# Two hybrid decoder layers on one core: the decay rate's group ahead of the receptance, a denser inverse, and a recurrence issued without gates

## The chip, the cores and the metric

The kernel runs on 1 core of one Trainium2 chip. The metric is the device time of one execution in microseconds (us). The engines are named as in the profile: PE is TensorE, DVE is VectorE, ACT is ScalarE, POOL is GpSimd, and SP issues most of the DMAs. PEld is TensorE's weight load.

## The reference

Two layers act on x of 256 tokens by 2048 features. Each layer makes one projection of x and splits its columns among three token mixers and their gates; the outputs go through one output projection, a residual and a layer norm.

```python
for l in range(DEPTH):
    u = x @ w_in[l]
    (cb, cc, ch, cg, cq, ckv, kpe, mg, rcols, rg) = _split(u, IN_SIZES)
    y_conv = _short_conv_branch(cb, cc, ch, cg, conv_w[l])
    y_mla = _mla_branch(cq, ckv, kpe, mg, ...)
    y_rwkv = _rwkv7_branch(rcols, rg, ...)
    mix = jnp.concatenate([y_conv, y_mla, y_rwkv], axis=-1)
    x = _layer_norm(DEEPNORM_ALPHA * x + mix @ w_out[l], ln_g[l], ln_b[l])
```

The third mixer, RWKV-7, is the one that the change is about. From rcols come the receptance r, the key k, the value v, a decay w and a removal rate a; 8 heads of 64 keep a 64x64 state each:

```python
def step(state, inp):
    r_t, w_t, k_t, v_t, a_t, b_t = inp
    sa = jnp.einsum('bhvk,bhk->bhv', state, a_t)
    state = (state * w_t[:, :, None, :] + sa[..., None] * b_t[:, :, None, :]
             + v_t[..., None] * k_t[:, :, None, :])
    return state, jnp.einsum('bhvk,bhk->bhv', state, r_t)
```

## The kernel before

**Projections.** The input projection is computed in groups of 512 columns, in the order of the tuple MAIN (k, r, a, v, cq, cc, ch, cb, cg, rg), later the two groups of LATE (mg). The group called a holds the inputs of decay and removal rate (64 columns each) with the latent key and value inputs. Apart from k, a group is two half-groups of 256 columns, and a half-group is four quarters of 16 matmuls (L437 and L439). Every weight is split into a high part (`hi_...`, a cast on ScalarE) and a low part (`lo_...`, a subtraction on VectorE); both are held in rings of four buffers, and the raw weights, which SP loads, in a ring of five. The accumulators of the groups (`u_...`, `pkv`, `pq`, `po`) share a ring of two.

**Ticks.** Other work is written as generators (rwkv, latent, conv). After each quarter, `tick` resumes every generator up to its next `yield`. While it does so, VectorE's instructions that are issued through the wrapper `V` are gated: `gates` makes each stand behind the low split of the weights two quarters ahead. `tc.high_priority(AHEAD)` and `tc.high_priority(EVICT)` rank instructions ahead of others. From these ranks and a timeline of its own, the scheduler sets the order on each engine.

**RWKV.** rwkv_k normalises the key (`kx`, `kkn`); rwkv_r makes the shifted receptance `rx`; rwkv_decay computes decay and rate with two small products (`pw`, `pa`, L569 and L570), a tanh each (`sig`, `tha`) and a scan (`cum`), from which `pe` and `pinv` come; rwkv_scale makes the scaled operands `kp`, `bk` and `ar`. The 256 tokens are four chunks of 64. rwkv_products multiplies within chunks (`pg`) and masks into `gs`. rwkv_inverse inverts 64 triangular blocks of 32x32: `gs` goes through DRAM into `bt`, then 31 steps of two VectorE instructions run (`tm`, then an addition into `xi`), and `xi` goes through DRAM into `xq`, is transposed (`xt1`) and merged into 64x64 inverses (`pz`, `zs`, `px`). rwkv_pairs (`pk`, `pv`, `pq` with `qs`) runs beside it.

rwkv_chain is the recurrence over chunks. For each chunk after the first it multiplies the state (`prh`), adds `qs` (`rhs`), multiplies by the inverse (`pu`) and copies the result into `uvt`, then makes the next state (`pst`, `st`); `out` makes the outputs of two chunks (`py`), which ScalarE copies to `y`. rwkv_norm begins with a sum over `y` (`gm`).

**Behind rg.** After rg the keys and values of the latent attention are expanded (mla_kv: `pkv`, evicted to `kn`, `vs`, `vt`), then the queries (mla_q: `pq`, `qn`, and `qp` by rope with the temporary `rt_q`), then mg is projected while mla_attend works head by head (`sc`, `ptr`, `po`).

Of the kernel before, what the change touches and what calls it, by code (L numbers as in the profile page):

```python
# [10 lines left out]
F32 = mybir.dt.float32  # L11
# [3 lines left out]
ALU = mybir.AluOpType  # L15
AX = mybir.AxisListType

P = 128
D = 2048
S = 256  # L20
# [4 lines left out]
AHEAD = 1500  # L25
EVICT = 4000
# [85 lines left out]
def hybrid_layers(ctx: ExitStack, tc: tile.TileContext, x, positions, xT, w_in, w_out, w_uq, w_ukv, par, wa_in, gb_in,  # L112
                  gbp, cst, eye32, sums, out):
    nc = tc.nc
# [8 lines left out]
    sm = ctx.enter_context(tc.tile_pool(name="sm", bufs=2))  # L123
    dr = ctx.enter_context(tc.tile_pool(name="dr", bufs=1, space=bass.MemoryType.DRAM))

    gates, splits = {}, []
# [18 lines left out]
    V, A, G, T = Gated(nc.vector, "V"), Gated(nc.scalar, "A"), nc.gpsimd, nc.tensor  # L145
# [151 lines left out]
    def until(name):  # L297
        while name not in done:
            yield
# [44 lines left out]
        for i, src in enumerate((hi, lo)):  # L344
            T.matmul(o, ones[:, which * P:which * P + P], src, start=i == 0, stop=i == 1)

    MAIN, LATE, ORDER = ("k", "r", "a", "v", "cq", "cc", "ch", "cb", "cg", "rg"), ("mg0", "mg1"), (0, 12, 4, 8)

    def acc(name):

# [126 lines left out]
    def rwkv(l, pq, u, t):  # L477
        yield from until(f"k{l}")
        yield from rwkv_k(l, pq, t, u["k"][0])
        yield from until(f"r{l}")  # L480
        yield from rwkv_r(l, pq, t, u["r"][0])
        yield from until(f"a{l}")
        yield from rwkv_decay(l, pq, t, u["a"][0][0])
        yield from rwkv_scale(l, pq, t)
        yield from rwkv_products(l, t)
        inv = rwkv_inverse(l, t)
        while f"v{l}" not in done:
            next(inv)
            yield
        yield from rwkv_v(l, pq, t, u["v"][0])  # L490
        fill = rwkv_pairs(l, t)
        while True:
            a, b = next(inv, "end"), next(fill, "end")
            if a == b == "end":
                break
            yield
        yield from rwkv_chain(l, t)
        done.add(f"chain{l}")
        yield from rwkv_norm(l, pq, t)
        yield from until(f"heads{l}")  # L500
        yield from rwkv_gate(l, t)
# [166 lines left out]
    def rwkv_inverse(l, st):  # L668
        gs = st["gs"]
        bd = dr.tile([64, 32, 32], F32, tag=f"bd{l}", name=f"bd{l}")  # L670
        for par in range(2):
            for k in range(2):
                r = slice(par * 64 + k * 32, par * 64 + k * 32 + 32)
                u0 = (par * 2 + k) * 16
                for i in range(2):
                    src = gs[i].rearrange("p c (b q) t -> p c b q t", q=2)[r, :, :, par, k * 32:k * 32 + 32]
                    nc.sync.dma_start(bd[u0 + 8 * i:u0 + 8 * i + 8].rearrange("(c b) i j -> i c b j", b=4), src)
        bt = s4(f"bt{l}", (64, 32, 32))
        nc.sync.dma_start(bt, bd)
        xi = s4(f"xi{l}", (64, 32, 32))  # L680
        after(nc.sync.dma_start(xi, eye32.rearrange("p (i j) -> p i j", j=32)), st["mark"])
        yield
        yield
        yield
        n = 0
        for j in range(31, 0, -1):
            w = 32 - j
            tm = sm.tile([64, j, w], F32, tag="rt", name=f"tm{l}_{j}")
            V.tensor_tensor(tm, bt[:, 0:j, j:j + 1].to_broadcast([64, j, w]),
                            xi[:, j:j + 1, j:32].to_broadcast([64, j, w]), ALU.mult)  # L690
            V.tensor_tensor(xi[:, 0:j, j:32], xi[:, 0:j, j:32], tm, ALU.add)
            n += 1
            if n == 3:
                yield
                n = 0
        xd = dr.tile([64, 32, 32], F32, tag=f"xd{l}", name=f"xd{l}")
        nc.sync.dma_start(xd, xi)
        xq = s4(f"xq{l}", (P, 4, 4, 64))
        xt1 = sm.tile([P, 4, 4, 32], F32, tag="s", name=f"xt1{l}")
        V.memset(xq, 0.0)  # L700
        yield
        for par in range(2):
            for k in range(2):
                r = slice(par * 64 + k * 32, par * 64 + k * 32 + 32)
                u0 = (par * 2 + k) * 16
                nc.sync.dma_start(xq[r, :, :, k * 32:k * 32 + 32],
                                    xd[u0:u0 + 16].rearrange("(c b) i j -> i c b j", b=4))
        yield
        yield
        for par in range(2):  # L710
            r = slice(par * 64, par * 64 + 32)
            t1 = V.transpose(xt1[r].rearrange("p c b t -> p (c b) t"), xq[r, :, :, 0:32].rearrange("p c b t -> p (c b) t"))
        yield
        zs = sm.tile([P, 16, 32], F32, tag="s", name=f"zs{l}")
        quarters = [(slice(par * 64, par * 64 + 32), slice(par * 64 + 32, par * 64 + 64)) for par in range(2)]
        pz = [pm.tile([P, 16, 32], F32, tag="m", name=f"pz{l}_{par}") for par in range(2)]
        for c in range(4):
            for b in range(4):
                for par, (ra, rb) in enumerate(quarters):
                    m = T.matmul(pz[par][rb, c * 4 + b, :], gs[c // 2][ra, c % 2, 2 * b + par, 32:64],  # L720
                                 xt1[ra, c, b, :], start=True, stop=True)
                    if c == b == par == 0:
                        gather(m, [t1])
        for par, (ra, rb) in enumerate(quarters):
            z1 = V.tensor_copy(zs[rb], pz[par][rb])
        yield
        px = [pm.tile([P, 16, 32], F32, tag="m", name=f"px{l}_{par}") for par in range(2)]
        for c in range(4):
            for b in range(4):
                for par, (ra, rb) in enumerate(quarters):  # L730
                    m = T.matmul(px[par][ra, c * 4 + b, :], zs[rb, c * 4 + b, :], xq[rb, c, b, 32:64],
                                 start=True, stop=True)
                    if c == b == par == 0:
                        gather(m, [z1])
        for par, (ra, rb) in enumerate(quarters):
            st["xq1"] = V.tensor_copy(xq[ra, :, :, 32:64].rearrange("p c b t -> p (c b) t"), px[par][ra])
        yield
        st["xq"] = xq
# [47 lines left out]
    def rwkv_chain(l, st):  # L786
# [28 lines left out]
        for c in range(4):  # L815
            cc = slice(c * 64, (c + 1) * 64)
            if state is None:
                rhs = qs[:, 0]
            else:
                pr_ = pm.tile([P, 4, 64], F32, tag="m", name=f"prh{l}_{c}")  # L820
                for b in range(4):
                    for par in range(2):
                        T.matmul(pr_[rs[par], b, :], ar[rs[par], b, 0, cc], state[rs[par], b, :], start=True, stop=True)
                rhs = slot("rhs", f"rhs{l}_{c}", (P, 4, 64), 2)
                V.tensor_tensor(rhs, pr_, qs[:, c], ALU.add)
                yield
            pu = pm.tile([P, 4, 64], F32, tag="m", name=f"pu{l}_{c}")
            for b in range(4):
                for par in (1, 0):
# [3 lines left out]
            moved = []  # L833
            for par in range(2):
                dst = uvt[:, c].rearrange("p (b q) t -> p b q t", q=2)[rs[par], :, par, :]
                if par == 0:
                    moved.append(V.tensor_copy(dst, pu[rs[par]]))
                else:
                    moved.append(A.copy(dst, pu[rs[par]]))
            yield  # L840
            if c < 3:
                pst = pm.tile([P, 4, 64], F32, tag="m", name=f"pst{l}_{c}")
                for b in range(4):
                    for par in (1, 0):
                        h = 2 * b + par
                        m = T.matmul(pst[rs[par], b, :], bkt[:, c, h, :], uvt[:, c, h, :], start=True, stop=True)
                        if b == 0 and par:
                            gather(m, moved)
                new = slot("st", f"st{l}_{c}", (P, 4, 64), 2)
                pc_ = pe[:, c::4, 64:65].to_broadcast([P, 4, 64])  # L850
                if state is None:
                    V.tensor_tensor(new, pst, pc_, ALU.mult)
                else:
                    V.tensor_tensor(new, pst, state, ALU.add)
                    V.tensor_tensor(new, new, pc_, ALU.mult)
            before.append(state)
            if c % 2:
                out(c // 2, before[-2:], moved)
# [196 lines left out]
    def mla_attend(l, st):  # L1055
# [4 lines left out]
        def split_queries(h):  # L1060
            t = qk[h % 2]
            split_in(t[:, 0, 0:P], t[:, 1, 0:P], qn[:, h, P:S])
# [3 lines left out]
            split_queries(h)  # L1066
            split_keys(st, h)

        split_queries(0)
        for par in range(2):  # L1070
            r, o = halves[par], halves[1 - par]
            of = lambda rr: q1.rearrange("p (g q) t -> p q g t", q=2)[rr, par]
            A.copy(of(r), qp[r, :, P:S])
            V.tensor_tensor(of(o), qp[r, :, P:S], of(r).bitcast(F32), ALU.subtract)
        split_queries(1)
        yield
        live = {}
        both = ((0, slice(0, 128)), (1, slice(128, 384)))

# [361 lines left out]
```

## Time and profile before

| | |
|---|---|
| median of 3 runs | 926.83 us (926.5 to 927.11) |
| profiled execution | 927.77 us |
| its span, first to last instruction | 926.0 us |
| mean granted clock of TensorE in it | 0.986 |
| busy: PE, DVE, ACT, POOL | 902.3, 690.7, 483.7, 22.7 us |
| HBM read, written | 158.61, 5.32 MB |

A busy time is a sum over the span, and an engine can be busy at a lower clock: the row PEclk of the profile gives the granted clock of TensorE in tenths, in 40 slices of the span, 9 standing for 90% or more. In a row of waits, the figures behind the colon are the sum in us over the execution, the number of times and the longest. In a row of a timeline, the first two figures are start and duration in us, the shapes are output and inputs, and the bracket gives the idle time of that engine just before and what ended it. In a row of windows, each engine has its busy time and its instructions, then come PEclk, the DMA engines' share and GB/s.

### The profile page before, as it was taken

To read this page: it belongs to the slowest core of one execution; us is meant where nothing else is said; L and a number is where in the kernel's file an instruction comes from. 1 tells how busy PE (TensorE), PEld (TensorE's weight loads), DVE (VectorE), ACT (ScalarE), POOL (GpSimd) and SP (SyncE) were. 2 spreads that over 40 slices of the span, in tenths; PEclk is the share of its full clock that TensorE was granted. 3 is DMA by queue.
4 is the path that set the end of the run, shared out by engine and by line. 5 is a ranking of instruction groups with operands and counts; after the bars stand their busy time and mean duration, and the time that the engine had idled before them with its cause. 6 is when DMAs were issued, how large, how long until landed. Compare 5 with 4: busy or idle time off the path is not lost.

```text
span 926.0 us, 15967 instructions
## 1 busy us (share of the span) xinstructions
PE 902.3 (97%) x6311; PEld 792.7 (86%) x6311; DVE 690.7 (75%) x1166; ACT 483.7 (52%) x750; POOL 22.7 (2%) x47
## 2 busy tenths in 40 slices
PE   8999999999989999999999999999999899999996
PEld 7888888888879888788898888888888898987896
DVE  6786898886548977566765778999865499763865
ACT  5756636444446566444246576464444366754430
POOL 1210000000000000000020000000000000000000
PEclk9999999999989999999999999999999799999998
DMA  9866465667434654596486664656664256546942
GB/s 319 257 177 213 122 188 163 178 185 202 149 86 122 192 160 137 158 343 206 159 227 185 185 181 147 185 142 190 191 178 142 70 160 189 151 136 191 338 131 91
DMA packets 67547, 164.97 MB, mean 178 GB/s; under 512 B 15430, under 2 KB 24694, under 8 KB 67462
## 3 DMA queue, kind: packets, MB, share of 16 engines
q1 hardware_dynamic: 59712, 150.36, 54.0%
q10 hardware_dynamic: 5072, 9.57, 3.1%
q0 software_dynamic: 2688, 4.03, 1.6%
q8 instruction: 49, 0.80, 0.4%
q14 instruction: 26, 0.21, 0.1%
HBM read 158.61 MB, written 5.32 MB: 177 GB/s over the span
## 4 chain that ended last, share of the span: by engine, by line
PE 90%; DVE 5%; ACT 1%; issue 1%; DMA 1%; SPq 0%; ACTq 0%; DVEq 0%
PE u_mg L437 6%; PE po L337 6%; PE po L338 6%; PE po L339 6%; PE u_rg L437 3%; PE u_cc L437 3%; PE u_cg L437 3%; PE u_cb L437 3%; PE u_mg L439 3%; PE u_ch L437 3%; PE u_v L437 3%; PE u_a L437 3%; PE u_cq L437 3%; PE u_r L437 3%; PE u_cc L439 2%; PE u_cg L439 2%
## 5 line engine op out<-in xcount | busy, mean ns | idle before, releaser
L138 DVE TENSOR_TENSOR lo_wo<-w_wo,hi_wo 128x1024 fp32r<-128x1024 f32 x57 | 69.2, 1222 | 52.0 <-ACT hi_wo L138 51.1
L138 ACT CAST hi_wo<-w_wo 128x1024 fp32r<-128x1024 f32 x57 | 59.6, 1053 | 65.4 <-PE po L339 49.2
L437 PE MATMUL u_mg<-x,hi_mg 128*128 128x512 f32 x256 | 90.8, 397 | 0.7 <-DVE rt_q L138 0.7
L439 PE MATMUL u_mg<-x,lo_mg 128*128 128x256 f32 x256 | 71.6, 280 | 0.0
L437 PEld LDWEIGHTS u_mg<-x,hi_mg 128*128 128x128 f32 x256 | 48.1, 188 | 11.7 <-issue 1.1
L337 PE MATMUL po<-hi_wo,ma 128*128 128x512 f32 (+1 forms) x128 | 46.8, 365 | 2.1 <-ACT ma L138 2.1
L439 PEld LDWEIGHTS u_mg<-x,lo_mg 128*128 128x128 f32 x256 | 48.3, 188 | 0.0
L138 ACT CAST hi_mg<-w_mg 128x1024 fp32r<-128x1024 f32 x32 | 33.6, 1050 | 26.5 <-PE pq L338 9.0
L339 PE MATMUL po<-hi_wo,ma 128*128 128x512 f32 (+1 forms) x128 | 46.6, 364 | 0.0
L437 PE MATMUL u_rg<-x,hi_rg 128*128 128x512 f32 x128 | 46.5, 404 | 0.0
L338 PE MATMUL po<-lo_wo,ma 128*128 128x512 f32 (+1 forms) x128 | 46.5, 363 | 0.0
L437 PE MATMUL u_cc<-x,hi_cc 128*128 128x512 f32 x128 | 46.5, 400 | 0.0
L437 PE MATMUL u_r<-x,hi_r 128*128 128x512 f32 x128 | 45.4, 397 | 0.9 <-DVE kx L138 0.9
L437 PE MATMUL u_cg<-x,hi_cg 128*128 128x512 f32 x128 | 45.7, 400 | 0.0
L138 DVE TENSOR_TENSOR lo_mg<-w_mg,hi_mg 128x1024 fp32r<-128x1024 f32 x32 | 39.1, 1221 | 8.8 <-ACT hi_mg L138 8.6
L437 PE MATMUL u_cb<-x,hi_cb 128*128 128x512 f32 x128 | 45.3, 399 | 0.0
L437 PE MATMUL u_ch<-x,hi_ch 128*128 128x512 f32 x128 | 45.3, 399 | 0.0
L437 PE MATMUL u_cq<-x,hi_cq 128*128 128x512 f32 x128 | 45.1, 396 | 0.0
L437 PE MATMUL u_v<-x,hi_v 128*128 128x512 f32 x128 | 44.9, 392 | 0.0
L437 PE MATMUL u_a<-x,hi_a 128*128 128x512 f32 x128 | 44.5, 391 | 0.0
L339 PE MATMUL u_k<-x,lo_k 128*128 128x256 f32 x128 | 36.6, 286 | 1.0 <-DVE lo_k L138 1.0
L337 PE MATMUL u_k<-x,hi_k 128*128 128x256 f32 x128 | 36.9, 288 | 0.6 <-ACT hi_k L138 0.6
(414 smaller groups left out, 2818.5 us busy)
## 6 DMA issues: line engine op xcount, KB each, us to landing
w_wo<-in_w_out_dram SPq DMA_DIRECT2D x64, 512.0 KB, 4.3
w_mg<-in_w_in_dram SPq DMA_DIRECT2D x32, 512.0 KB, 4.2
w_r<-in_w_in_dram SPq DMA_DIRECT2D x16, 512.0 KB, 5.6
w_a<-in_w_in_dram SPq DMA_DIRECT2D x16, 512.0 KB, 3.8
w_v<-in_w_in_dram SPq DMA_DIRECT2D x16, 512.0 KB, 4.0
w_cq<-in_w_in_dram SPq DMA_DIRECT2D x16, 512.0 KB, 3.7
w_cc<-in_w_in_dram SPq DMA_DIRECT2D x16, 512.0 KB, 3.9
w_ch<-in_w_in_dram SPq DMA_DIRECT2D x16, 512.0 KB, 3.8
```

Of the source, the lines that this page charges most:

```text
L138: inst = call(*args, **kwargs)
L337: m = T.matmul(o, lh, rh, start=first, stop=False, skip_group_check=True)
L338: T.matmul(o, lh, rl, start=False, stop=False, skip_group_check=True)
L339: T.matmul(o, ll, rh, start=False, stop=last, skip_group_check=True)
L437: T.matmul(ps[:, b, :].rearrange("p (i t) -> p i t", i=2), hi[:, k, c], x2, start=k0 + k == 0, stop=False, skip_group_check=True)
L439: T.matmul(ps[:, b, 0:S], lo[:, k, c], x2[:, 0, :], start=False, stop=k0 + k == NKC - 1, skip_group_check=True)
```

## The change

MAIN has the group a ahead of r, and rwkv runs rwkv_decay ahead of rwkv_r. The inverse does five steps between two yields, where it did three, and its `tm` is taken from the pool tag "s" (which `xt1` and `zs` use) and no longer from "rt" (which the norms' temporaries use). In the recurrence the yield behind `rhs` is gone, so a chunk takes two ticks where it took three, and its VectorE instructions are issued on the engine itself, without the gate, at priority EVICT. In mla_attend the gates are cleared for the first tick, and the splits of the first queries are ranked AHEAD.

```diff
-    MAIN, LATE, ORDER = ("k", "r", "a", "v", "cq", "cc", "ch", "cb", "cg", "rg"), ("mg0", "mg1"), (0, 12, 4, 8)
+    MAIN, LATE, ORDER = ("k", "a", "r", "v", "cq", "cc", "ch", "cb", "cg", "rg"), ("mg0", "mg1"), (0, 12, 4, 8)
...
         yield from rwkv_k(l, pq, t, u["k"][0])
+        yield from until(f"a{l}")
+        yield from rwkv_decay(l, pq, t, u["a"][0][0])
         yield from until(f"r{l}")
         yield from rwkv_r(l, pq, t, u["r"][0])
-        yield from until(f"a{l}")
-        yield from rwkv_decay(l, pq, t, u["a"][0][0])
...
-            tm = sm.tile([64, j, w], F32, tag="rt", name=f"tm{l}_{j}")
+            tm = sm.tile([64, j, w], F32, tag="s", name=f"tm{l}_{j}")
...
-            if n == 3:
+            if n == 5:
                 yield
...
-                V.tensor_tensor(rhs, pr_, qs[:, c], ALU.add)
-                yield
+                with tc.high_priority(EVICT):
+                    nc.vector.tensor_tensor(rhs, pr_, qs[:, c], ALU.add)
...
-                if par == 0:
-                    moved.append(V.tensor_copy(dst, pu[rs[par]]))
-                else:
-                    moved.append(A.copy(dst, pu[rs[par]]))
+                with tc.high_priority(EVICT):
+                    moved.append((A.copy if par else nc.vector.tensor_copy)(dst, pu[rs[par]]))
...
-                if state is None:
-                    V.tensor_tensor(new, pst, pc_, ALU.mult)
-                else:
-                    V.tensor_tensor(new, pst, state, ALU.add)
-                    V.tensor_tensor(new, new, pc_, ALU.mult)
+                with tc.high_priority(EVICT):
+                    if state is None:
+                        nc.vector.tensor_tensor(new, pst, pc_, ALU.mult)
+                    else:
+                        nc.vector.tensor_tensor(new, pst, state, ALU.add)
+                        nc.vector.tensor_tensor(new, new, pc_, ALU.mult)
...
-        split_queries(0)
-        for par in range(2):
...
-        split_queries(1)
-        yield
+        gates.clear()
+        with tc.high_priority(AHEAD):
+            for par in range(2):
...
+                split_queries(par)
```

The change moves instructions on all engines. At three places the order reads as follows; the number behind a name's first underscore is the layer's or the chunk's, and the last number only tells tiles apart.

TensorE at the end of the recurrence in layer 0. Before, behind the second group of keys and values, the last steps stand one after another:

```order
L338 MATMUL pkv0_1_2968<-lo_ukv0_1_0_2884,hkv0_1481 128x256
L339 MATMUL pkv0_1_2968<-hi_ukv0_1_0_2883,hkv0_1481 128x256
L846 MATMUL pst0_2_2439<-uvt0_1554,bkt0_1458 64x64 x8
L823 MATMUL prh0_3_2473<-st0_2_2448,ar0_1058 64x64 x8
L830 MATMUL pu0_3_2506<-rhs0_3_2482,xq0_1979 64x64 x8
L799 MATMUL py0_1_0_2542<-uvt0_1554,gs0_1_1166 64x64 x8
```

Now `pst` of chunk 2 stands 22 matmuls of rg earlier, and `prh` of chunk 3 comes at the beginning of the first group:

```order
L437 MATMUL u_rg0_1_2814<-x0_3_85,hi_rg0_1_12_2839 128x512
L439 MATMUL u_rg0_1_2814<-x0_3_85,lo_rg0_1_12_2840 128x256
L337 MATMUL pkv0_0_2933<-hkv0_1561,hi_ukv0_0_0_2861 128x256
L338 MATMUL pkv0_0_2933<-hkv0_1561,hi_ukv0_0_0_2861 128x256
L339 MATMUL pkv0_0_2933<-hkv0_1561,lo_ukv0_0_0_2862 128x256
L823 MATMUL prh0_3_2281<-st0_2_2249,ar0_988 64x64 x8
```

`pu` of chunk 3 follows 21 matmuls of that group later, and `py` behind the 24 of the second.

ScalarE behind the recurrence, where it evicts the first two groups of keys and values (`vs`, `vt`) and the last outputs (`y`). Before:

```order
L138 CAST vs0_2926<-pkv0_0_2933 128x256
L138 CAST vs0_2926<-pkv0_1_2968 128x256
L138 COPY vt0_2925<-pkv0_0_2933 128x256
L138 COPY vt0_2925<-pkv0_1_2968 128x256
L138 COPY y0_2190<-py0_1_0_2542 128x4x64
L138 COPY y0_2190<-py0_1_1_2543 128x4x64
L138 ACTIVATE gsq0_2605<-y0_2190 128x1024
```

Now:

```order
L138 CAST vs0_2926<-pkv0_0_2933 128x256
L138 CAST vs0_2926<-pkv0_1_2968 128x256
L138 COPY y0_2039<-py0_1_0_2331 128x4x64
L138 COPY y0_2039<-py0_1_1_2332 128x4x64
L138 COPY vt0_2925<-pkv0_0_2933 128x256
L138 COPY vt0_2925<-pkv0_1_2968 128x256
L138 ACTIVATE gsq0_2396<-y0_2039 128x1024
```

The two copies of `y` have moved ahead of the two of `vt`.

VectorE in the inverse of layer 0, between two low splits of weights. Before, in ch:

```order
L138 TENSOR_TENSOR lo_ch0_1_8_1924<-w_ch0_1_8_1921,hi_ch0_1_8_1923 128x1024
L138 TENSOR_TENSOR tm0_17_1789<-bt0_1454,xi0_1456 64x255
L138 TENSOR_TENSOR xi0_1456<-xi0_1456,tm0_17_1789 64x17x15
L138 TENSOR_TENSOR tm0_16_1815<-bt0_1454,xi0_1456 64x256
L138 TENSOR_TENSOR lo_ch0_1_12_1955<-w_ch0_1_12_1952,hi_ch0_1_12_1954 128x1024
```

Now, in cc:

```order
L138 TENSOR_TENSOR lo_cc0_1_8_1697<-w_cc0_1_8_1694,hi_cc0_1_8_1696 128x1024
L138 TENSOR_TENSOR tm0_22_1598<-bt0_1387,xi0_1389 64x220
L138 TENSOR_TENSOR xi0_1389<-xi0_1389,tm0_22_1598 64x22x10
L138 TENSOR_TENSOR tm0_21_1646<-bt0_1387,xi0_1389 64x231
L138 TENSOR_TENSOR xi0_1389<-xi0_1389,tm0_21_1646 64x21x11
L138 TENSOR_TENSOR tm0_20_1649<-bt0_1387,xi0_1389 64x240
L138 TENSOR_TENSOR xi0_1389<-xi0_1389,tm0_20_1649 64x20x12
L138 TENSOR_TENSOR lo_cc0_1_12_1740<-w_cc0_1_12_1737,hi_cc0_1_12_1739 128x1024
```

Three steps stand between two splits where there was one and a half, and the same steps come in an earlier group.

More of the change, by code (lines that the diff above doesn't have):

```diff
@@ L1067, in split_qk @@
             split_keys(st, h)
-        split_queries(0)
-        for par in range(2):
[L1071 to L1074, printed above, removed]
-        split_queries(1)
-        yield
+        gates.clear()
+        with tc.high_priority(AHEAD):
+            for par in range(2):
+                r, o = halves[par], halves[1 - par]
+                of = lambda rr: q1.rearrange("p (g q) t -> p q g t", q=2)[rr, par]
+                A.copy(of(r), qp[r, :, P:S])
+                V.tensor_tensor(of(o), qp[r, :, P:S], of(r).bitcast(F32), ALU.subtract)
+                split_queries(par)
         live = {}
```

## The prediction

> **What bounds the kernel now.** I read the page first, then who waits on TensorE, then TensorE's timeline where the waits lie, then the granted clock in half-microsecond windows there. The page's head:
>
> ```profile
> span 926.0 us, 15967 instructions
> PE 902.3 (97%) x6311; PEld 792.7 (86%) x6311; DVE 690.7 (75%) x1166; ACT 483.7 (52%) x750; POOL 22.7 (2%) x47
> PEclk9999999999989999999999999999999799999998
> ```
>
> TensorE is busy 97% of the span, so at most 23.7 us of idle time are to be had. But the clock row dips twice inside (0.8 and 0.7 of a slice of 23 us), and there a busy TensorE works at half speed. The waits of TensorE, both layers summed:
>
> ```profile
> PE prh L823 <- DVE st L138: 3.5, 2, 1.7
> PE u_cq L439 <- DVE lo_cq L138: 1.3, 2, 0.7
> PE pu L830 <- DVE rhs L138: 1.1, 2, 0.5
> ```
>
> Two of them belong to the recurrence (prh, pu). They lie where its last chunk comes after the last half-group of the gate, rg, with nothing left to put between the steps. TensorE there, layer 0, columns start, duration, instruction:
>
> ```profile
> 261.70 0.28 PE L337 MATMUL pkv<-hkv,hi_ukv 128*128 128x256 f32 x1
> 261.82 0.28 PE L338 MATMUL pkv<-hkv,hi_ukv 128*128 128x256 f32 x1
> ...
> 268.35 0.69 PE L846 MATMUL pst<-uvt,bkt 128*64 128x64 f32 x16
> 270.76 0.68 PE L823 MATMUL prh<-st,ar 64*64 64x64 f32 x16 [1.73 <-DVE st L138]
> 271.97 1.02 PE L830 MATMUL pu<-rhs,xq 64*64 64x64 f32 x16 [0.53 <-DVE rhs L138]
> 272.92 1.71 PE L799 MATMUL py<-uvt,gs 128*64 128x64 f32 x18
> ...
> 277.83 0.58 PE L337 MATMUL pkv<-hkv,hi_ukv 128*128 128x256 f32 x1 [0.28 <-ACT vt L138]
> ...
> 301.27 0.35 PE L337 MATMUL pq<-hq,hi_uq 128*128 128x256 f32 x1 [0.26 <-DVE rt_q L138]
> ...
> 306.18 0.47 PE L437 MATMUL u_mg<-x,hi_mg 128*128 128x512 f32 x1 [0.37 <-DVE rt_q L138]
> ```
>
> A pkv matmul starts every 0.12 us at 261.7. And the clock (first column the window, the figure behind POOL is PEclk):
>
> ```profile
> 272.00:272.50 0.50, 0.50 (x12) 0.50 (x14) 0.00 (x0) 0.00 (x0) 0.40 (x1) 0.62 0.82 326
> 282.00:282.50 0.50, 0.50 (x5) 0.50 (x4) 0.00 (x0) 0.50 (x1) 0.00 (x0) 0.64 0.00 0
> 729.50:730.00 0.50, 0.11 (x4) 0.00 (x0) 0.34 (x1) 0.00 (x0) 0.00 (x0) 0.51 0.96 197
> 739.50:740.00 0.50, 0.50 (x5) 0.50 (x5) 0.14 (x1) 0.27 (x1) 0.00 (x0) 0.75 0.00 0
> 390.00:392.00 2.00, 0.94 (x5) 0.44 (x4) 1.20 (x2) 1.89 (x3) 0.00 (x0) 1.00 0.73 170
> ```
>
> In each layer the clock falls to 0.50 right after the recurrence's waits. With the share of the edge windows it is low from about 272.2 to 282.4 and from 729.5 to 739.8, 10.2 us each. At 390 to 392, TensorE is idle for half of the window and the clock stays at 1.00.
>
> [...]
>
> **The change, part by part.** The profiled execution took 927.77 us with a span of 926.0; it stands 0.94 over the median of the runs, 926.83. The sum is made against 927.77 and then lowered by 0.94.
>
> *The tail.* The rate's group before the receptance, five steps of the inverse a tick and one tick less a chunk bring the recurrence forward. In the new order pu and pst of chunk 2 lie in rg, 22 matmuls of rg and 3 of pkv stand between pst and prh of chunk 3, 21 of pkv between prh and pu, 24 between pu and py. From the first pkv to u_mg the time is 306.18 - 261.70 = 44.48 us. Idle in it: 1.73 + 0.53 + 0.28 + 0.26 + 0.37 = 3.17. Half speed: 10.24 less the 0.28 is 9.96, of which 4.98 are lost. Most that can be won: 8.15 a layer. pu and pst (1.3 us) only change their place on TensorE.
>
> What is late next: the accumulator of the third pkv is free when ScalarE has copied vt out, and the new order puts the two y copies, which wait for py, ahead of vt (before, behind it):
>
> ```profile
> 277.41 0.70 ACT L138 COPY vt<-pkv 128x256 f32<-128x256 f32 x2 [0.22 <-DVE vs L138]
> 278.00 0.65 ACT L138 COPY y<-py 128x256 f32<-128x256 f32 x2
> ```
>
> From rg's end at 0, TensorE does 3 pkv, prh, 21 pkv, pu, 24 pkv (48 x 0.12 = 5.76, and 0.65 twice) and the 64 py, which took 277.55 - 272.92 = 4.6 at half clock, so 2.2 (estimate): done at 9.2. y to 9.9, first vt to 10.3: a wait of 1.1. Then VectorE: it begins the norm (gm) on y, and its rt_q releases u_mg:
>
> ```profile
> 278.69 1.22 DVE L138 TENSOR_REDUCE gm<-y 128x16 f32<-128x1024 f32 x1 [0.99 <-ACT y L138]
> ...
> 304.31 1.72 DVE L138 TENSOR_TENSOR rt_q<-pq,sinT 32x256 f32<-32x256 f32 x4
> ```
>
> That is 306.03 - 278.69 = 27.34, nearly all busy. In the new order two splits of qn (0.4) stand earlier in it, and less is lost to TensorE's slow clock. From gm at 10.0 it ends between 36.6 (less 0.99 that TensorE's two slow groups cost it, plus the 0.4, which I estimate at 26.6) and 37.8 (all 27.34 and the 0.4). TensorE's own work from 10.3 (two pkv groups, four pq groups, pt and sc: 306.18 - 277.83, less 2.3 for the 4.6 us at half clock and 0.63 of waits, 25.4) ends at 35.7. So TensorE still waits for rt_q there, by up to 1; I put u_mg at 36.8. Without pu and pst, which now precede rg's end, the time before was 44.48 - 1.3 = 43.2: 6.4 won a layer. Ends: 5.2 (VectorE's path in full, u_mg at 38.0) and 8.15.
>
> *The early part.* Today VectorE waits for kp and is then late with a split:
>
> ```profile
> 95.62 0.69 DVE L138 TENSOR_SCALAR sig<-sig 128x1024 f32<-128x1024 f32 x1
> 96.34 2.29 DVE L138 TENSOR_TENSOR_SCAN cum<-cum,sig 128x1024 f32<-128x1024 f32 x1
> ...
> 99.63 1.04 ACT L138 ACTIVATE pinv<-cum 128x1024 f32<-128x1024 f32 x1
> 100.58 2.07 ACT L138 ACTIVATE kp<-tha,pc 128x256 f32<-128x256 f32 x4
> 102.68 1.23 DVE L138 TENSOR_TENSOR kp<-kp,kx 128x1024 f32<-128x1024 f32 x1 [2.93 <-ACT kp L138]
> ...
> 111.66 0.39 PE L439 MATMUL u_cq<-x,lo_cq 128*128 128x256 f32 x1 [0.61 <-DVE lo_cq L138]
> ```
>
> Now three splits and the shift of r stand between the scan and kp on VectorE, so the 2.93 are filled, and 0.61 and 0.7 of TensorE's waits go: 1.3 in all, ends 0 and 1.3. Where cover is thin: on ScalarE hi_v of the third quarter of v now stands behind pe, pinv (1.04 each), two rx (0.9) and four kp (2.07). From the start of r's second half at 0, the last lora product ends at 6.9 (28 of 64 matmuls at 2.83 a quarter, 2 us of products), ScalarE's tanh at 7.5, scaling and scan at 10.5, those eight at 15.5, hi at 16.5, lo at 17.7. TensorE asks at 11.3 + 2.0 + 2 x 2.83 = 19.0, or 18.7 with its start: 1.0 to spare. I take no wait; ends 0 and 1.7 a layer (as late as today's split, and the 1.0 lost). On SP the stores of the masks and the load of bt and xi come earlier too; bt lands some 4 us ahead of the first step (issue to landing 5.2), so no queue waits for it.
>
> *The inverse.* A quarter of a half-group lasts 202.00 - 199.17 = 2.83 us on TensorE; VectorE runs ahead by 199.17 - 192.89 = 6.3 in steady state, and by 159.60 - 148.17 = 11.4 where the products stand among the group's matmuls:
>
> ```profile
> 146.94 1.23 DVE L138 TENSOR_TENSOR lo_cc<-w_cc,hi_cc 128x1024 fp32r<-128x1024 f32 x1 [0.26 <-ACT hi_cc L138]
> 159.60 0.28 PE L439 MATMUL u_cc<-x,lo_cc 128*128 128x256 f32 x1
> 191.66 1.23 DVE L138 TENSOR_TENSOR lo_cb<-w_cb,hi_cb 128x1024 fp32r<-128x1024 f32 x1 [0.68 <-ACT hi_cb L138]
> 199.17 0.28 PE L439 MATMUL u_cb<-x,lo_cb 128*128 128x256 f32 x1
> 202.00 0.28 PE L439 MATMUL u_cb<-x,lo_cb 128*128 128x256 f32 x1
> 173.87 0.42 DVE L138 TENSOR_TENSOR tm<-bt,xi 64x256 f32<-64x256 f32 x1
> ```
>
> Five widest steps are ten instructions of about 0.42, and with the split 1.2 they make 5.4 us against 2.83. In the new order the six splits from the second half of cc on (6.9) stand with the steps of columns 27 to 16 (24 instructions of about 0.4, 9.6) and some 20 for the norms of kv and q (8.7, estimated from these durations by width): 25.2 us of VectorE against six quarters, 17.0, of TensorE. 8.2 lost from a lead of 11.4 leaves 3.2. No wait, no cost; the other buffer for tm takes only the coupling to the norms' temporaries away. The inverse then ends five quarters, 14 us, earlier than it did.
>
> *Its way out.* After the last step VectorE's transposes wait for two DMAs:
>
> ```profile
> 210.42 0.17 DVE L138 TENSOR_TENSOR xi<-xi,tm 64x31 f32<-64x31 f32 x1
> 217.87 0.70 DVE L138 STREAM_TRANSPOSE xt<-xq 32x512 f32<-32x512 f32 x1 [2.41 <-DMA xq<-xd]
> 220.23 1.41 PE L720 MATMUL pz<-xt,gs 32*32 32x32 f32 x64
> ```
>
> 7.3 us from step to transpose. The new order puts pz 10 matmuls into the last quarter of cb, a split and cy between the two transposes; counted so, pz waits 0.5 a layer (ends 0 and 1.3). The ungated splits for the queries change VectorE's order only behind u_mg's release, and the 0.4 is counted.
>
> Sum: 2 x 6.4 + 1.3 - 2 x 0.5 = 13.1. 927.77 - 13.1 = 914.7, less 0.94 is 913.7; I say 914.
>
> **Rivals.**
> *The clock falls all the same.* In the window before pkv's third group TensorE has only short 64-wide matmuls and the 1.1 us wait. If that counts as too little, 10.24 us at half speed follow where TensorE and VectorE are about level: 5.1 less the 0.7 waited anyway, 4.4 a layer: 914 + 8.8 = 922.8. For it: it fell there with waits of 2.3. Against: 1.06 idle in 2 at 390 did not do it.
> *VectorE is crowded out by the inverse, and it gets slower.* Place: the first splits of ch. If VectorE is later than I count, by over 3.2 us of the 25.2, TensorE waits for lo_ch. From a wait of about 1.7 the clock falls too (the 1.73 above), in a stretch bound by TensorE: for 3.4 of waiting 3.4 + 5.1 = 8.5 a layer, 914 + 17 = 931. Against: that takes a quarter more work than the rows give (6.6 of 25.2).
> *The recurrence is no earlier in fact,* as pz, pu and pst each wait for their way out in cg and rg: what leaves the tail comes back there, 926.8.
>
> **How the numbers follow.** Forecast 0.70, between 909.2 (8.15 twice and 1.3 won, nothing lost) and 922.4 (5.2 twice, less 1.3 and 1.7 twice, won: 4.4). Clock 0.13. No gain 0.05. Slower 0.09. Better than 909 0.03. Leaving out the last three leaves 0.17, so the range is 909 to 923. A measurement here tells 0.2%, 1.9 us, from no change: faster 0.86, same 0.05, slower 0.09.
>
> **What would show it.** Right: PEclk 1.00 in every slice but the last; no wait of prh or pu; a wait of pkv for vt or y of about 1 us; no u_cq wait; the span of pkv to u_mg 36 to 38 us. Wrong: half clock anywhere else, waits of u_v, u_cc or u_ch for their lo, or u_mg released by VectorE later than 38 us after rg.

## The result, and the profile after

The changed kernel takes 917.28 us (median of 4 runs, 917.22 to 918.24) against 926.97 beside it: a ratio of 0.989, 95% interval 0.9865 to 0.9915. It is faster by about 10 us; 914.0 was forecast, with 909 to 923 as the range. The profiled execution took 917.24 us, 10.5 less than the one of before (927.77). A ratio in this document compares executions made beside each other and is not the quotient of the two medians; where the two differ a little, the ratios are compared.

The head of the page, then rows of the waits of TensorE (both layers summed; sum, times, longest):

```profile
span 915.5 us, 15974 instructions
PE 895.2 (98%) x6311; PEld 787.3 (86%) x6311; DVE 688.3 (75%) x1166; ACT 485.9 (53%) x753; POOL 24.7 (3%) x47
PEclk9999999999999999999999999999999999999998
```

```profile
PE pkv L337 <- ACT vt L138: 2.9, 2, 1.4
PE u_mg L437 <- DVE rt_q L138: 2.0, 2, 1.6
```

Both inner dips of PEclk are gone, and so are the waits of prh, pu and u_cq. What stands in their place is the wait of the third pkv group for vt, and a longer one of u_mg. TensorE in layer 0:

```profile
263.09 0.28 PE L337 MATMUL pkv<-hkv,hi_ukv 128*128 128x256 f32 x1
...
263.55 0.68 PE L823 MATMUL prh<-st,ar 64*64 64x64 f32 x16
...
266.86 0.68 PE L830 MATMUL pu<-rhs,xq 64*64 64x64 f32 x16
...
270.54 1.15 PE L799 MATMUL py<-uvt,gs 128*64 128x64 f32 x32
...
273.75 0.38 PE L337 MATMUL pkv<-hkv,hi_ukv 128*128 128x256 f32 x1 [1.43 <-ACT vt L138]
...
300.84 0.47 PE L437 MATMUL u_mg<-x,hi_mg 128*128 128x512 f32 x1 [0.37 <-DVE rt_q L138]
```

From the first pkv to u_mg it is 37.75 us (44.48 before); in layer 1, from 715.43 to 753.46, 38.03 (44.18 before). From the start of k to the first pkv of layer 1 it is 258.86 us (715.43 - 456.57) against 257.47 (719.87 - 462.40), 1.39 more; pu and pst of chunk 2 stand there now, and each makes the step from one matmul of rg to the next 0.71 longer, 1.42 together. So nearly all of the gain lies in the tail.

### The profile page after: what moved, and what is told of

Its sections match the earlier page's. It is cut to its first block, busy times and chain, and to the rows that moved or that the text cites. A ratio compares the mean times of both kernels' runs of the same rounds, so it can differ in the third digit from the quotient of the medians.

```text
span 915.5 us, 15974 instructions
## 1 busy us (share of the span) xinstructions
PE 895.2 (98%) x6311; PEld 787.3 (86%) x6311; DVE 688.3 (75%) x1166; ACT 485.9 (53%) x753; POOL 24.7 (3%) x47
## 4 chain that ended last, share of the span: by engine, by line
PE 92%; DVE 4%; ACT 1%; issue 1%; DMA 1%; SPq 0%; ACTq 0%; DVEq 0%
PE u_mg L437 7%; PE po L337 6%; PE po L338 6%; PE po L339 6%; PE u_cc L437 3%; PE u_rg L437 3%; PE u_cg L437 3%; PE u_mg L439 3%; PE u_v L437 3%; PE u_cb L437 3%; PE u_cq L437 3%; PE u_ch L437 3%; PE u_r L437 3%; PE u_a L437 3%; PE u_rg L439 2%; PE u_cg L439 2%
```

## The experiments

Two readings stood against each other after the result. Both count on the order of the groups. B is the prediction's: beside it, five steps of the inverse between two yields and one tick less a chunk bring the recurrence forward, and the other buffer is a side matter. A was formed from TensorE's order in kernels with one part undone: the buffer of tm and the order of the groups do it.

**The buffer back.**

```diff
-            tm = sm.tile([64, j, w], F32, tag="s", name=f"tm{l}_{j}")
+            tm = sm.tile([64, j, w], F32, tag="rt", name=f"tm{l}_{j}")
```

> The changed kernel with one line back: the temporary of the inverse comes from the ring of two that the norms of kv and q use. Theory A, formed after the result: that ring is what held the inverse back; without the other buffer its steps begin three splits later, the last three chunk steps stand back to back behind the second group of keys and values again, prh and pu of chunk 3 wait 1.7 and 0.5 us as before, pst of chunk 2 a further 0.5 to 1, the clock falls to 0.5 for 10 us in each layer: 925 to 931 us. Theory B, the prediction's: five steps between two yields bring the recurrence forward and the other buffer adds next to nothing: 917 to 919 us, no half clock inside.

Measured: 927.22 us, ratio to before 0.9992 (0.9982 to 1.0002). With everything else of the change in place, all of the gain is gone. TensorE in layer 0 there:

```profile
268.80 0.69 PE L844 MATMUL pst<-uvt,bkt 128*64 128x64 f32 x16 [0.92 <-ACT uvt L138]
270.56 0.81 PE L823 MATMUL prh<-st,ar 64*64 64x64 f32 x16 [1.08 <-DVE st L854]
271.89 1.12 PE L830 MATMUL pu<-rhs,xq 64*64 64x64 f32 x16 [0.52 <-DVE rhs L826]
```

pst, prh and pu stand back to back again, with 2.5 us of waits, and PEclk has its two dips again (the mean granted clock is 0.986, as before). Where the inverse begins and ends says why. VectorE's first step of the kernel before, with the instruction ahead of it (its last addition into xi, at 210.42, stands in the prediction):

```profile
150.23 0.42 DVE L138 SCALAR_TENSOR_TENSOR sumq<-nw_q,sumq 128x256 f32<-128x256 f32 x1
150.57 0.19 DVE L138 TENSOR_TENSOR tm<-bt,xi 64x31 f32<-64x31 f32 x1
```

The first step and the last addition of the changed kernel:

```profile
134.54 0.19 DVE L138 TENSOR_TENSOR tm<-bt,xi 64x31 f32<-64x31 f32 x1
...
195.31 0.18 DVE L138 TENSOR_TENSOR xi<-xi,tm 64x31 f32<-64x31 f32 x1
```

And of this run, with a stretch of the middle:

```profile
143.81 0.42 DVE L138 SCALAR_TENSOR_TENSOR sumkv<-nw_kv,sumkv 128x256 f32<-128x256 f32 x1
144.15 0.19 DVE L138 TENSOR_TENSOR tm<-bt,xi 64x31 f32<-64x31 f32 x1
...
166.11 0.41 DVE L138 TENSOR_TENSOR xi<-xi,tm 64x255 f32<-64x255 f32 x1
...
171.91 0.42 DVE L138 TENSOR_SCALAR nv_q<-prsq 128x256 f32<-128x256 f32 x1 [1.20 <-PE prsq L345]
...
174.81 0.41 DVE L138 TENSOR_TENSOR tm<-bt,xi 64x256 f32<-64x256 f32 x1
...
215.28 0.18 DVE L138 TENSOR_TENSOR xi<-xi,tm 64x31 f32<-64x31 f32 x1
```

In the program the norms of kv and q take their temporaries (`nv_`, `nw_` and others) from the same ring of two, so a step cannot have its own before a norm is done, and the norms wait for TensorE and ScalarE in between (1.20 us for prsq above, 2.46 us for sumkv at 142.89). Before, the first step stands right behind the norm of q. Here it stands behind the norm of kv, and for 8.7 us, while the norm of q runs, no step begins. So the inverse begins 6.4 us earlier than before, but takes 71.1 us and not 59.9, and ends 20 us later than with the change, where it takes 60.8. Reading A holds.

**Three steps again.**

```diff
-            if n == 5:
+            if n == 3:
```

> The changed kernel with three steps of the inverse between two yields, as before. Theory A (the buffer and the order of the groups do it): pz some 5 us later, prh of chunk 3 four pkv matmuls later, pu 17 matmuls behind it, no wait of prh or pu, clock 1.00 in the tail: 916.5 to 918.5 us. Theory B (five steps do it): the recurrence falls back behind the second group of keys and values, waits and half clock come back: 922 to 927 us.

Measured: 916.58 us, ratio 0.9879 (0.9855 to 0.9904): the same as the change within the intervals, and its profile is 915.17. So the five steps, the first of the two parts on which reading B rests, win nothing. They cost a little: pz in the changed kernel, then here.

```profile
205.30 2.31 PE L720 MATMUL pz<-xt,gs 32*32 32x32 f32 x64
```

```profile
208.49 1.35 PE L720 MATMUL pz<-xt,gs 32*32 32x32 f32 x64
```

And the second transpose on VectorE, in the changed kernel:

```profile
205.66 0.70 DVE L138 STREAM_TRANSPOSE xt<-xq 32x512 f32<-32x512 f32 x1
```

With five steps pz begins before the second of the two transposes has ended, and its 64 matmuls take 2.31 us with the wait among them; with three it comes 3 us later, behind both, and takes 1.35.

**The order of the groups undone.**

```diff
-    MAIN, LATE, ORDER = ("k", "a", "r", "v", "cq", "cc", "ch", "cb", "cg", "rg"), ("mg0", "mg1"), (0, 12, 4, 8)
+    MAIN, LATE, ORDER = ("k", "r", "a", "v", "cq", "cc", "ch", "cb", "cg", "rg"), ("mg0", "mg1"), (0, 12, 4, 8)
...
+        yield from until(f"r{l}")
+        yield from rwkv_r(l, pq, t, u["r"][0])
         yield from until(f"a{l}")
         yield from rwkv_decay(l, pq, t, u["a"][0][0])
-        yield from until(f"r{l}")
-        yield from rwkv_r(l, pq, t, u["r"][0])
```

> The changed kernel with r ahead of a again. Here pst of chunk 2 stands among the matmuls of pkv's first group and prh of chunk 3 behind the second, 30 matmuls (3.6 us) later, so that prh no longer waits, while pu follows prh directly and waits for rhs (0.5 to 0.9). u_cq waits for its low split again, 1.3 in all. If a wait of 0.5 to 0.9 among 64-wide matmuls is enough for the clock to fall: 10 us at half speed in each layer, 922 to 925 us. If the fall needs the 1.7 us wait ahead of it: no half clock, and the tail some 0.5 us a layer longer than with the change: 918 to 920.5 us.

Measured: 923.07 us, ratio 0.995 (0.993 to 0.997). TensorE in layer 0:

```profile
269.83 0.68 PE L823 MATMUL prh<-st,ar 64*64 64x64 f32 x16
271.04 0.68 PE L830 MATMUL pu<-rhs,xq 64*64 64x64 f32 x16 [0.53 <-DVE rhs L826]
...
272.70 0.69 PE L799 MATMUL py<-uvt,gs 128*64 128x64 f32 x16 [0.72 <-DVE uvt L837]
...
275.92 0.39 PE L337 MATMUL pkv<-hkv,hi_ukv 128*128 128x256 f32 x1 [0.71 <-ACT vt L138]
```

prh waits for nothing, but pu, py and pkv do, 2 us in 5. In this profile the clock stays at 1.00 all the same (every slice of PEclk has a 9, and the mean is 0.998), and yet pkv to u_mg takes 40.5 and 40.75 us (263.20 to 303.70, 718.09 to 758.84), some 2.7 more than with the change and not 0.5. The expectation had the wait of pu and left out those that follow from it on the same short chain, of py for uvt and of the accumulators for vt, and the later y. The two tails are 5.5 us longer together and the whole span 4.5 (920.0 against 915.5), so all of it lies there; the 1.3 of u_cq is made up by other differences.

The medians lie 5.8 apart, and there the clock comes in after all. Of the eight executions the profiled one has a mean granted clock of 0.998, and the two longest, 926.78 and 925.97 us, have 0.986 and 0.991. No trace of those two was kept, but 0.986 is what the kernel before has with its two falls. So the granted clock differs between executions of one and the same kernel; that it falls behind these waits in the long ones is a reading of the means, not shown by a trace.

**The gates back, the queries' splits as before.** The hunks of rwkv_chain and mla_attend are undone:

```diff
-                with tc.high_priority(EVICT):
-                    nc.vector.tensor_tensor(rhs, pr_, qs[:, c], ALU.add)
+                V.tensor_tensor(rhs, pr_, qs[:, c], ALU.add)
+                yield
...
-        gates.clear()
...
+        split_queries(1)
+        yield
```

> Only the order of the groups, the buffer and the five steps; the recurrence is gated and takes three ticks a chunk, and the queries' splits are issued as before. TensorE's order up to the third pkv group is that of the change. Theory A: these two parts win nothing by themselves; the two splits of qn (0.4 us of VectorE ahead of the last rope) are even out of the way: 916.5 to 917.8 us. The rival, that the missing gates are what lets VectorE answer the recurrence in time: prh or pu wait again, and with them the clock falls: 920 to 927 us.

Measured: 917.18 us, ratio 0.989 (0.9864 to 0.9915). These two parts win nothing by themselves.

**The buffer alone**, in the kernel before:

```diff
-            tm = sm.tile([64, j, w], F32, tag="rt", name=f"tm{l}_{j}")
+            tm = sm.tile([64, j, w], F32, tag="s", name=f"tm{l}_{j}")
```

> The kernel before with one line changed: the inverse's temporary from the other ring. Theory A: the inverse begins three splits earlier, TensorE's order at the end of the recurrence is that of the run with r ahead of a (prh of chunk 3 thirty matmuls behind pst), so no half clock inside, and about 40 us from pkv to u_mg: 921.5 to 924 us. Rival (the buffer only helps together with five steps): 925.5 to 927.5 us, with the half clock.

Measured: 923.84 us, ratio 0.994 (0.9918 to 0.9963). One line brings about half of the gain, as much as the whole change without the order of the groups (0.995, above). The order on top of it brings the rest, and without the buffer it brings nothing (the first experiment). The two are links of one chain: the buffer takes away the wait of the inverse for the norms, the order brings the inverse's input earlier. No run has just these two: five steps were taken out alone, and the ungated recurrence with the queries' splits alone, so that one of them could stand in for the other is not excluded. Alone, the buffer lets the inverse begin at 147.08, 3.5 us earlier than before and not three splits (8.5), since it waits there for the load of xi, which stands behind the products:

```profile
147.08 0.20 DVE L138 TENSOR_TENSOR tm<-bt,xi 64x31 f32<-64x31 f32 x1 [1.47 <-DMA xi<-in_eye_dram]
```

The expectation of no half clock inside failed, and the run shows the clock at its margin. Both layers have the same waits of pu and py; layer 0, then layer 1:

```profile
271.76 0.68 PE L830 MATMUL pu<-rhs,xq 64*64 64x64 f32 x16 [0.53 <-DVE rhs L138]
...
273.42 0.69 PE L799 MATMUL py<-uvt,gs 128*64 128x64 f32 x16 [0.72 <-DVE uvt L138]
...
729.33 0.68 PE L830 MATMUL pu<-rhs,xq 64*64 64x64 f32 x16 [0.53 <-DVE rhs L138]
...
730.99 0.69 PE L799 MATMUL py<-uvt,gs 128*64 128x64 f32 x16 [0.72 <-DVE uvt L138]
```

And the windows behind them (the figure after POOL is the granted clock):

```profile
274.00:274.50 0.50, 0.50 (x18) 0.47 (x14) 0.00 (x0) 0.00 (x0) 0.00 (x0) 0.98 1.34 147
274.50:281.00 6.50, 6.23 (x56) 5.81 (x53) 3.38 (x5) 2.09 (x7) 0.00 (x0) 0.50 0.13 52
281.00:281.50 0.50, 0.50 (x5) 0.50 (x5) 0.00 (x0) 0.50 (x1) 0.00 (x0) 0.69 0.00 0
732.00:739.00 7.00, 6.29 (x80) 6.01 (x77) 3.47 (x6) 3.04 (x8) 0.00 (x0) 1.00 0.14 48
```

In layer 0 the clock fell to 0.50 for 6.8 us, and the pkv matmuls in that stretch start 0.21 us apart, where it is 0.12 at 1.00; at the same place of layer 1 it did not fall at all. From pkv to u_mg it is 41.85 and 40.47 us.

**The waits of the kernel before, filled.** Before, with matmuls that nothing reads in the two gaps:

```diff
+        def keep_busy(l, i, n, m, dm=None):
...
+            for _ in range(n):
+                d = T.matmul(dm, ones[:, 0:P], ones, start=True, stop=True)
...
+                            dm, last = keep_busy(l, 0, 14, m_)
...
+                        dm, last = keep_busy(l, 1, 5, m_, dm)
```

> The kernel before, with 14 matmuls (128x256, into an accumulator that nothing reads) between pst of chunk 2 and prh of chunk 3, and 5 between prh and pu: TensorE works through the two waits of 1.73 and 0.53 us and nothing else changes. If the waits are what lowers the clock: 1.00 throughout, pu and py at full speed, y some 3 us earlier, and since VectorE needs its 27 us from gm to the last rope, u_mg some 3.4 us earlier in each layer: 919 to 921.5 us. If the clock falls for another reason (the 64-wide matmuls themselves): half speed for 10 us as before, 926 to 928 us.

Measured: 924.15 us, ratio 0.996 (0.9943 to 0.9976); the profile's span is 921.4 against 926.0. TensorE in layer 0, then PEclk of the page and a row of the waits:

```profile
268.83 1.93 PE L819 MATMUL fill<-ones 128*128 128x256 f32 x14
270.69 0.68 PE L835 MATMUL prh<-st,ar 64*64 64x64 f32 x16
271.30 0.86 PE L819 MATMUL fill<-ones 128*128 128x256 f32 x5
272.09 0.68 PE L847 MATMUL pu<-rhs,xq 64*64 64x64 f32 x16
```

```profile
PEclk9999999999999999999999999999999999999998
```

```profile
PE u_mg L437 <- DVE rt_q L138: 2.9, 2, 1.4
```

Work that has no use makes the kernel faster: without the waits of prh and pu the clock stays at 1.00 (the mean is 0.997), so in this run the 64-wide matmuls alone did not lower it. But pkv to u_mg became only 2.3 and 2.0 us shorter (42.15 in both layers), not the 4.98 that was worked out as lost to half speed, nor the 3.4 expected, and 924.15 misses the 919 to 921.5: u_mg now waits 1.4 us for rt_q. Counted from the first pkv, VectorE begins gm at 14.89 where it began at 16.99 and 17.08, not 3 us earlier, and then needs 27.1 us (27.3 and 27.0 before). TensorE at full speed is ahead of VectorE, and VectorE sets the end.

**What binds the tail now.** Two edits of the changed kernel. In the first, the split of mc is made later, which leaves a free buffer to vs, whose split and the copy of vt behind it then need not wait for py:

```diff
-        yield from until(f"chain{l}")
+        yield from until(f"mg0{l}")
```

> The changed kernel, in which the split of the convolution's output (mc) waits until the first half of mg is done. Its buffer, that of gs, then goes to kn and that of bkt to vs, so vs and vt of the first pkv group no longer wait for py: the 1.43 us wait of the third pkv group should go. Theory (VectorE's path from gm to the last rope sets u_mg): y is copied some 0.5 us earlier, u_mg comes 0.4 to 0.6 earlier in each layer, TensorE's wait moves to u_mg behind rt_q (1.3 to 2.2 in each layer): 915.9 to 916.9 us. Rival (TensorE's own path sets u_mg): the 1.43 us are won in each layer: 914 to 914.8 us.

In the second, the third rope stands ahead of the second split of mg's weights on VectorE:

```diff
+        if name[:3] == "mg0" and name[4:] == "_0_4":
+            after(ops[1], mark["rope"])
```

> The changed kernel, in which the second split of mg's weights stands behind the third rope on VectorE (before, two splits of 1.2 us stand ahead of it). Theory (VectorE's path sets u_mg, and TensorE has 0.4 us left in layer 0 and 1.6 in layer 1): u_mg is released 1.2 us earlier, 0.4 won in layer 0 and 1.2 in layer 1: 915.4 to 916.2 us. Rival: another release (the accumulator's copies on ScalarE, a later split) holds u_mg: 916.8 to 917.6 us.

> The two edits of the last two runs together. Theory: TensorE's path is 1.43 us shorter and VectorE's 1.6 in each layer, so u_mg comes 1.4 to 1.65 us earlier in each: 913.8 to 914.7 us. Rival (one path alone binds): as the better of the two alone, 915.4 to 916.5 us.

Measured: the late mc alone 920.29 us, ratio 0.9923 (0.9898 to 0.9948), against 0.989 of the change it is not better, and rather worse, outside both its expectations; the rope ahead 916.77, 0.9883 (0.9868 to 0.9899); both 915.27, 0.987 (0.9853 to 0.9887). From pkv to u_mg: 37.43 in both layers with the late mc, 37.21 and 37.22 with the rope, 36.28 in both with the two (37.75 and 38.03 with the change). The wait of pkv for vt is gone with the late mc, but what TensorE wins there it loses a little later, at u_mg, in one piece, and the clock falls. TensorE in layer 0, and the windows:

```profile
301.00 0.47 PE L437 MATMUL u_mg<-x,hi_mg 128*128 128x512 f32 x1 [2.24 <-DVE rt_q L138]
```

```profile
301.00:301.50 0.50, 0.50 (x3) 0.46 (x4) 0.50 (x1) 0.00 (x0) 0.00 (x0) 1.00 0.90 369
301.50:302.00 0.50, 0.50 (x4) 0.40 (x3) 0.50 (x1) 0.00 (x0) 0.00 (x0) 0.54 0.27 107
302.00:304.50 2.50, 2.50 (x9) 2.11 (x9) 2.47 (x6) 0.00 (x0) 0.00 (x0) 0.50 0.49 116
304.50:305.00 0.50, 0.50 (x4) 0.40 (x3) 0.47 (x2) 0.00 (x0) 0.00 (x0) 0.55 0.91 360
```

A clock of 0.50 for 3.4 us; by that share 1.7 of them are lost (estimate). In layer 1 u_mg waits as long (4.5 us in both layers together), and the mean granted clock of the profile, 0.993 against 0.996 with the change, leaves room for a second such fall (0.003 of 917.8 us, doubled, is 5.5 us, more than one fall takes; estimate). With the rope ahead as well, u_mg's wait is 1.1 us in each layer and the mean is 0.996. With the rope alone u_mg waits for nothing, so TensorE's path sets it, and with both edits it is VectorE's again: the theory that VectorE's path from gm to the rope sets u_mg holds for the changed kernel, but TensorE's path ends only 0.4 us ahead of it in layer 0 and 1.6 in layer 1. Counted from the first pkv to the end of the layer, the profiles are below the change's by 0.3 us (layer 0) and 1.1 (layer 1) with the rope and by 1.3 and 1.9 with both, near what was expected. The medians missed their expectations by 0.6 each: 915.4 to 916.2 with the rope, where 916.77 lies at the edge of the rival's 916.8, and 913.8 to 914.7 with both. The intervals of the rope alone and of the change overlap, so that it is faster is shown by the profiles' tails alone.

**The parts together**: `if n == 3` and the two edits above, or `if n == 3` and the rope alone, beside the changed kernel on one chip.

> The changed kernel with three steps of the inverse between two yields, the late split of mc and the third rope ahead of the second split of mg. If the parts add up: 0.8 us a layer from pz, which with three steps doesn't wait for the transposes, and 1.6 a layer from the two edits of the tail: 4 to 5 us below the change in the profile, 2.5 to 5 in the median. If they share a path (a later recurrence eats what the tail wins): 1 to 2.5 below it.

> The changed kernel itself beside the others on one chip: 916.5 to 918.5 us, no wait of prh or pu, 1.4 us of pkv for vt in each layer.

> The changed kernel with three steps of the inverse between two yields and the third rope ahead of the second split of mg, mc split as early as with the change. Against the change: 0.8 us a layer from pz, 0.4 and 1.2 from the rope: 2.5 to 3.5 us below it, 914 to 915 us; 1 to 2 us above the run with the late mc as well, unless the late split of mc costs elsewhere what it wins.

Measured: 913.45 us with three steps, late mc and rope, ratio to before 0.9836 (0.9821 to 0.9852); 914.69 with three steps and the rope, 0.9859 (0.9837 to 0.9882); the changed kernel 919.47 there, 0.9901 (0.988 to 0.9921), its profile at 917.47 with the same waits as above. In the profiles the parts add up: 2.1 us with three steps and 1.6 with the two edits of the tail, each against the first profile of the change, and 3.7 together here, a little under the 4 to 5 expected. The medians lie 6.0 and 4.8 us below the change's, more than expected (2.5 to 5, and 2.5 to 3.5), because the change itself came out 1 us above its expected 918.5. The first of the three beats both kernels: its interval lies clear below the change's.

## Why the prediction was right, and where it was wrong

**The clock.** Right. In the profiles the dips are gone, and filling the waits alone removes them too. The rival that it falls all the same did not happen, but it was near: of four places with waits of 0.53 and 0.72 us among short matmuls, it fell behind one, and it fell behind the 2.24 us wait of u_mg in layer 0 with the late mc; behind the waits of 1.43 and 1.62 in the changed kernel's profile it did not (PEclk is 1.00 from 270.61 to 274.02 and from 751.89 to 755.30 us). When the changed kernel was run again, two of its four executions, 919.93 and 920.88 us, had a mean granted clock of 0.993 where the profiled one had 0.997: if it is half speed that is missing, some 13 us of the 918 and not 5 (estimate: the share missing from 1, doubled), at places of which no trace was kept.

**What brings the recurrence forward.** Wrong, though the sum did not suffer, since the order was read from the new program as a whole. "The rate's group before the receptance, five steps of the inverse a tick and one tick less a chunk bring the recurrence forward", and the other buffer "takes only the coupling to the norms' temporaries away". That coupling was what held the inverse. Five steps bring nothing, and one tick less brings nothing (916.58 and 917.18 without them, each taken out alone); the buffer alone brings about half of the gain, and the order on top of it the rest. That the order was read off, and not worked out from the mechanism, is why the wrong cause cost the forecast nothing.

**The tail, 6.4 us a layer.** Mis-sized. Measured by the same rule it is 44.48 - 37.75 - 1.42 = 5.3 and 44.18 - 38.03 - 1.42 = 4.7, together 2.8 short (0.3 of it because 44.48 was taken for both layers). The terms that were too small are VectorE's path and, beside it, TensorE's. ScalarE, then VectorE in layer 0:

```profile
272.38 0.67 ACT L138 COPY y<-py 128x256 f32<-128x256 f32 x2
```

```profile
271.99 0.96 DVE L138 TENSOR_TENSOR lo_uq<-w_uq,hi_uq 128x768 fp32r<-128x768 f32 x1 [2.71 <-ACT hi_uq L138]
272.87 0.75 DVE L138 TENSOR_TENSOR vs<-pkv,vs 128x256 fp32r<-128x256 f32 x2
273.53 1.21 DVE L138 TENSOR_REDUCE gm<-y 128x16 f32<-128x1024 f32 x1
...
295.80 2.36 DVE L138 TENSOR_TENSOR lo_mg<-w_mg,hi_mg 128x1024 fp32r<-128x1024 f32 x2
...
298.97 1.72 DVE L138 TENSOR_TENSOR rt_q<-pq,sinT 32x256 f32<-32x256 f32 x4
```

y is copied by 9.96 us after rg's end, as worked out, but gm begins at 10.4, not 10.0: VectorE first has to make a low split of the queries' weights and the low parts of vs, which stand ahead of gm and are late themselves (2.71 us of waiting). With the late mc, where one low part of vs comes earlier, gm begins at 10.06. From gm to the end of rt_q it takes 27.2 us here and 27.4 in layer 1, not the 26.6 that was estimated. The sum given for it, 27.34 less 0.99 plus 0.4, makes 26.75; the rest is the 0.99, for which no row was given. VectorE is busy for 24.75 of the 27.34 us before and for 25.12 of 27.16 now, so its idle time fell by only 0.55, while its work grew by 0.37, near the 0.4. Two splits of mg stand ahead of the last rope, as they did before; moving one behind it made the tail 0.5 and 0.8 shorter. The upper end given there, 37.8, was about right, and the value taken was too hopeful. TensorE's own path, which was to end at 35.7, ends at 37.4 and 36.4: these are u_mg's starts less its waits of 0.37 and 1.62. The wait of pkv for vt was put at 1.1 and is 1.43.

**The early part.** u_cq no longer waits, 1.3 won as said. The third quarter of v has 1.45 us to spare (its low split ends at 84.52, its first matmul is at 85.97), where 1.0 was worked out. Not foreseen: the products (pg) take 0.9 and 0.8 us longer from first to last. They now come where VectorE also shifts v between two of their maskings, and TensorE's weight load waits for one twice a layer (1.0 us in four waits, both layers); that this is all of it is not shown.

**The inverse's lead.** The smallest lead of VectorE over ch in layer 0 is 3.3 us, where 3.2 was worked out: the third split of ch ends at 164.36 and TensorE asks for it at 167.66. The rival that the inverse crowds VectorE out did not happen.

**pz.** 0.5 a layer was put down; it is 0.9 and 0.74, and three steps avoid it.

**The 0.94 between profile and median.** It was taken off on both sides, but the profile after (917.24) lies at its own median, so that the gain by medians, 9.6, is less than by the profiles, 10.5. From 913.7 to 917.24 it is 3.5 us: this 0.9, the tail's 2.8 and 0.2 of the early part, less 0.4 won behind u_mg. In the early part 0.1 was won and not 0.3: the 1.3 of u_cq stands against 1.8 more for pg and 1.6 more for pz, and smaller differences, which are not taken apart here, make up the rest.

## What to carry to other kernels

A chain of small dependent steps that takes its temporaries from a ring shared with other work runs at that work's pace: look who else uses the ring before asking how densely the chain is issued, and undo the parts of a change one at a time, since the part that looks like the point may be the idle one. Where TensorE has waits and short matmuls within a few us, read the granted clock behind them, and in more than one execution (behind 0.53 and 0.72 us of waits it fell at one place here and not at three), but price the fall by the engine that ends last there (VectorE here, which left 2 of the 5 us). A wait removed on such a path can move down the path, as the 1.43 us of pkv did to u_mg, and in one long piece (2.24 us) it can cost more than before (920.29 us against 917.28).

## What was not expected of the hardware

By the share of the edge windows, the falls of the clock last 10.24 us (before, both layers), 6.83 (the buffer alone, layer 0) and 3.41 (the late mc, layer 0): three, two and one times 3.41. The same waits of 0.53 and 0.72 us were followed by a fall once (the buffer alone, layer 0) and not another three times. With the late mc the clock fell behind a single wait of 2.24 us, and the matmuls on both sides of it (`sc` and u_mg) are 128 to 512 wide, not 64.

In the profile of before, the clock changes at 272.12, 282.36, 729.51, 739.75 and 920.66 us, that is 3, 131, 3 and 53 times 3.413 us apart. The span can so be cut into steps of this length. In the two steps that end in a fall, TensorE is busy for 1.16 and 1.68 us, 34 and 49%:

```profile
268.71:272.12 3.41, 1.16 (x32) 0.88 (x30) 2.05 (x4) 1.69 (x3) 0.08 (x1) 1.00 0.56 139
726.10:729.51 3.41, 1.68 (x37) 1.37 (x35) 1.62 (x3) 1.91 (x3) 0.00 (x0) 1.00 0.43 118
```

The matmuls that begin in them have 1536 and 2560 columns (a 128x256 counted as 256, a 64x64 as 64). Up to 880 us, no other step at full clock there has less than 72% or fewer than 2944 columns. In the changed kernel, cut in the same way from its one change at 908.90 us, the lowest are 54% and 3840, and none ends in a fall. The 54% are in the step with u_mg's wait of 1.62 us in layer 1:

```profile
751.89:755.30 3.41, 1.84 (x11) 1.65 (x12) 3.34 (x6) 1.93 (x6) 0.00 (x0) 1.00 0.72 272
```

So in these two profiles both measures tell the steps ahead of a fall from the others; that either is the cause is not shown, since no run moved the steps against the waits.
